# Hybrid decoder trunk: sums of weights formed in the first layer only, sums of h stored by GpSimd and loaded later, last weight pieces of the first layer at another priority

## The chip, the cores and the metric

The kernel runs on one core of a Trainium2 chip. The metric is the device time of one execution in microseconds (us), from the run's own timer; the value given is the median of several runs. The profile is of one more execution, recorded by the hardware profiler. PE is TensorE (matmuls), DVE is VectorE, ACT is ScalarE, POOL is GpSimd, and SP is SyncE, which here only issues DMA transfers. All five run their own list of instructions in order and wait for each other by semaphores.

## The reference

Two decoder layers on 512 tokens of width 1024, each followed by h = LayerNorm(alpha * h + sublayer(h)). In short:

```python
# layer 0 (even): one projection x @ w_in, cut into q, k, v, g_ret, xb, g_lru
ret = retention(rope(q), rope(k) * dk ** -0.5, v)        # 8 heads, per-head decay
ret = group_norm(ret) * gn_g + gn_b
ret = ret * silu(g_ret)
lru = rg_lru(causal_conv(xb)) * silu(g_lru)              # gated linear recurrence
y0 = concat([ret, lru]) @ w_out
# layer 1 (odd): h @ w_in, cut into q, k, v, g
p = softmax(q @ k.T, causal)                             # 8 heads, two maps each
out = (p1 - lam * p2) @ v
out = rms_norm(out) * subln_g * (1 - lambda_init) * silu(g)
y1 = out @ w_out
```

Everything is float32.

## The kernel before

**Precision.** Each float32 operand is split into a high part and a low part (`split`: a cast on ACT, a subtraction on DVE), and each product is three matmuls: high x high, high x low, low x high (`mm3`, L152). PE therefore runs some 4,255 matmuls, most of 128x128 by 128x512, and each weight piece needs a cast on ACT and a subtraction on DVE before PE can use it.

**Weight pieces.** The weights come in 162 pieces of 128x1024 (512 KB) in the order of use, w0, w1, and so on (`order`). `fetch` loads the next piece through SP into one of a few raw buffers (three in the first layer, four in the second), splits it into one of five pairs of buffers (the first two pieces of the second layer, w64 and w65, have a pair of their own each), and appends it to `ready`. `take(ahead)` returns the next piece and makes sure that `ahead` more have been fetched. w4 to w57 and v's pieces are projections of the first layer; w58 and w59 are the output projection of a retention pair ("ro"), and w60 to w63 of the last pairs ("eo"). w64 to w67 are the second layer's v, w68 to w71 its g, w72 to w79 its first q and k.

**Sums of weights.** In the second layer the gate and the value projections of head pairs 1 to 3 are done together by a scheme of Strassen's kind: seven products of half-size blocks in place of eight (`gates_values`). It needs sums of weight blocks, formed in HBM: for each, SP copies one block to `t` (L180), and GpSimd's queue adds another by a DMA that accumulates (L181). 24 sums of 128x1024, in halves of 64 rows, make 48 pairs of transfers. `fetch` issues one pair behind a weight piece n if `n >= SUM_FIRST and n % 3 != SUM_REST`, that is behind two pieces of three.

**Sums of h.** The same scheme needs four sums of blocks of h. `act_sums` makes them on DVE and ACT while PE does g of the second layer, and stores their high and low parts to HBM (`sd`, eight stores of 512 KB, L720). They are loaded later into `sx`, two at a time (`load_sum`, L743). `sx` shares its buffer with `y`, the residual sum, so that y is stored first (`store_y`, L701), `sx` loaded for a group, and y loaded again for the next output projection. The list `later` says when: `qk_unit` (one projection of a q or k, followed by its rope) takes one entry after each unit.

**Order.** PE's and SP's instructions stand in the order of the program text (`manual_schedule`), with side jobs (retention, recurrence, attention, layer norm) put between matmuls by `Side.tick`. The order on DVE, ACT and POOL is made by the compiler's scheduler, in which `tc.high_priority(n)` moves what is recorded inside it ahead by n. The pieces of the second layer's v are taken with priority `P_WEIGHTS` = 450 (L209).

**At the seam.** "eo" is the first layer's last output unit: for each of four row blocks, w60 and w61 with the recurrence's results (lrum3), then w62 and w63 with the retention's (retm3). After each row block, `even_end` does its layer norm on DVE, and later four by four transposes on PE (ht, L601) make h. Then come v (ov_ps), g (og_ps), and the units q00o, q01o, k00o, k01o, q10o and so on. Each is 24 matmuls.

Of the kernel before, what the change touches and what calls it, by code (L numbers as in the profile page):

```python
# [42 lines left out]
WARM_UP = 7  # L43
EARLY = 2

SUM_FIRST, SUM_ROWS, SUM_REST = 6, 64, 0

ATT_BUSY = 1

# [51 lines left out]
def trunk(ctx: ExitStack, tc: tile.TileContext, a):  # L101
    nc = tc.nc
# [64 lines left out]
    def fetch(parts=((0, D),)):  # L167
        if len(ready) < len(order):
            n = len(ready)
            src, scale = order[n]  # L170
            raw = raws[n % len(raws)].tile([P, D], F32, tag="raw", name=f"w{n}_r")
            w = pair(extra.pop(n, wsp), [P, D], "w", f"w{n}")
            for lo, hi in parts:
                c = slice(lo, hi)
                nc.sync.dma_start(out=raw[:, c], in_=src[:, c])
                split(raw[:, c], cut(w, ALL, c), scale=scale)
                yield
            if n >= SUM_FIRST and n % 3 != SUM_REST and sums:
                dst, one, two = sums.pop(0)
                nc.sync.dma_start(out=dst, in_=one)  # L180
                nc.gpsimd.dma_start(out=dst, in_=two, max_dma_last_dim=4 * D, accum_op=ALU.add)  # L181
            ready.append(w)
# [3 lines left out]
    def take(ahead):  # L186
        taken[0] += 1
        while len(ready) < min(taken[0] + ahead, len(order)):
            list(fetch())
        return ready[taken[0] - 1]  # L190

    def t_unit(act, name):
        w = take(2)
        ps = bank(ps_pj, "pj", name + "_ps")
        for kt in range(KT):
            mm3(ps, cut(w, ALL, slice(kt * P, kt * P + P)), cut(act, ALL, kt), kt == 0, kt == KT - 1)
            side.tick()
        return ps
# [25 lines left out]
                for sb, j in steps:  # L224
                    product(ps[sb], w, sb, 2 * i + j)

    def out_unit(mix, y, name, first, before=None, after=None, late=0):
        n = len(mix)
        w = [take(1 if n == 2 else 0) for _ in range(n)]
        y = y()  # L230

        step = 2 if n == 4 and after is None else 1
        for sbs in (range(i, i + step) for i in range(0, SB, step)):
            pss = {(sb, hf): bank(ps_pj, "pj", f"{name}_ps{sb}{hf}") for sb in sbs for hf in range(2)}
            steps = [(c, sb, hf) for c in range(0, n, 2) for sb in sbs for hf in range(2)]
            if late and sbs[0] == SB - 1:
                steps.sort(key=lambda t: t[2])
            for c, sb, hf in steps:
                if before is not None and hf == 0:
                    before(c // 2, sb)  # L240
                ps = pss[sb, hf]
                for i in range(c, c + 2):
                    mm3(ps, cut(mix[i], ALL, slice(sb * P, sb * P + P)), cut(w[i], ALL, slice(hf * HALF, hf * HALF + HALF)), i == 0, i == n - 1)
                    side.tick()
                if c < n - 2:
                    continue
                yy = y[:, sb, hf * HALF:hf * HALF + HALF]
                with tc.high_priority(late):
                    if first:
                        nc.vector.scalar_tensor_tensor(out=yy, in0=yy, scalar=ALPHA, in1=ps, op0=ALU.mult, op1=ALU.add)  # L250
                    else:
                        nc.vector.tensor_tensor(out=yy, in0=ps, in1=yy, op=ALU.add)  # L252
                    if late:
                        if hf == 0:
                            st = small.tile([P, 2, 6], F32, tag="bst", name="bst", bufs=2)
                        nc.vector.bn_stats(out=st[:, hf], in_=yy)
                        stats[sb] = st
                if after is not None and hf:
                    after(sb)
# [22 lines left out]
    sums = []  # L282
# [266 lines left out]
    def even_out(kinds, p, name, **kw):  # L549
        def before(c, sb):  # L550
            if sb == 0:
                for i in range(2):
                    side.need(job[kinds[c], 2 * p + i])

        out_unit([t for kind in kinds for t in mix_of(m.pop((kind, p)))], lambda: y, name, p == 0, before=before, **kw)
# [51 lines left out]

    hj = []
    gb0 = ln_params(a["ev_ln"], "ln0", (two, "dec"), (two, "dec"), (two, "gwh", 1), (two, "gwl", 1))
    even_out(("lru", "ret"), 3, "eo", after=even_end)  # L610


    phase.close()
# [92 lines left out]
    def act_sums():  # L706
        def block(r, c, x):
            return h[x][:, 4 * c:4 * c + 4, 2 * P * r:2 * P * r + 2 * P].bitcast(F32)

        def less(t, one, two, three):  # L710
            nc.vector.scalar_tensor_tensor(out=t, in0=one, scalar=-1.0, in1=two, op0=ALU.mult, op1=ALU.subtract)
            yield 2
            nc.vector.tensor_tensor(out=t, in0=t, in1=three, op=ALU.subtract)
            yield 1

        def put(n):
            split(low[n], (st[n][:, 0].bitcast(F32R), low[n].bitcast(F32R)))
            yield 3
            for x in range(2):
                nc.sync.dma_start(out=sd[n][:, x], in_=st[n][:, x])  # L720

        def difference(t, one, two):
            nc.vector.tensor_tensor(out=t, in0=block(*one, 0), in1=block(*two, 0), op=ALU.subtract)
            yield 2
            nc.vector.tensor_tensor(out=t, in0=t, in1=block(*one, 1), op=ALU.add)
            yield 1
            nc.vector.tensor_tensor(out=t, in0=t, in1=block(*two, 1), op=ALU.subtract)
            yield 2

        st = [ss.tile([P, 2, KT // 2, 2 * P], F32, tag=f"ss{n}", name=f"ss{n}") for n in range(4)]  # L730
        low = [t[:, 1] for t in st]
        yield from difference(low[0], (1, 1), (1, 0))
        yield from less(low[1], low[0], block(0, 0, 0), block(0, 0, 1))
        yield from put(0)
        yield from less(low[3], low[1], block(0, 1, 0), block(0, 1, 1))
        yield from put(1)
        yield from put(3)
        yield from difference(low[2], (0, 0), (1, 0))
        yield from put(2)
# [81 lines left out]
                for qb in range(SB):  # L821
                    side.need(oj[hd, qb])

    later, busy = [], [0]

    def no_op():
        pass

    def swap_in():
        nonlocal sx  # L830
# [1 line left out]
        load_sum(1, 0)  # L832
        load_sum(2, 1)

    def qk_unit(n, name):
        r = rope(t_unit(h, name), n, name)
        if later:
            later.pop(0)()
        return r

    sx = None
# [2 lines left out]
    for kind, i in od:  # L844
        if kind == "v":
            vs[i] = []

            def evac(sb, ps):
                past(i - 1)
                t = pair(vp, [P, S], "v", f"ov{i}{sb}")  # L850
                split(ps, t)
                vs[i].append(t)

            s_unit(h, f"ov{i}", i == 0, evac, lambda sb: side.need(hj[sb]))
            vt[i] = side.now + ATT_VALUE
            if i == 0:
                early.close()
                scratch = ctx.enter_context(ExitStack())
                ss = pool("ss", 1, scratch)
                summed = side.add(act_sums(), "sums", 1)  # L860
        elif kind == "g":
            def evac(sb, ps):
                past(i - 1)
                if sb % 2 == 0:
                    pairs[sb] = gp.tile([P, 2, S], F32, tag="g", name=f"og{i}{sb}")
                gates[sb, i] = pairs[sb - sb % 2][:, sb % 2]
                silu2(ps, gates[sb, i], work(f"og{i}{sb}_t"))

            pairs = {}
            s_unit(h, f"og{i}", False, evac)  # L870
            side.need(summed)
            scratch.close()
            qkp = pool("qkp2", 4)
            es = pool("es2", 2)
            mask = load("mask", [P, S], a["mask"], pl=es, bufs=1)
            later[:] = [store_y, no_op, swap_in]
        elif kind == "gv":
            gates_values(i)
        elif kind == "qk":
            om[i] = mix_pair(f"om{i}") if i < 7 else None  # L880
            qk = [[qk_unit(n, f"{n}{i}{mp}o") for mp in range(2)] for n in "qk"]
            om[i] = om[i] or cut(pair(big, [P, KT, S], "x", "om7"), ALL, slice(0, 2))
            for qb in range(SB):
                oj[i, qb] = side.add(attention(i, qb, *qk, om[i]), "att", 3, ATT_START[i], ATT_GAP[i])
        else:
            odd_out(i, f"oo{i[0]}")
            if i[0] < 4:
                later[:] = [store_y, no_op, swap_in]
    gb1 = ln_params(a["od_ln"], "ln1", *((qkp, n) for n in ("qh", "ql", "kh", "kl")))
    odd_out((6, 7), "oo6", after=odd_end, late=P_LAST)  # L890

# [82 lines left out]
```

## Time and profile before

| | us |
|---|---|
| median of 3 runs (941.3 to 943.25) | 942.57 |
| the profiled execution, its own time | 941.73 |
| its span, first to last instruction | 939.9 |
| idle time of PE up to 360 us (of 340 from 20) | 1.6 |
| longest wait of PE for another engine | 2.7 |

The profile page gives, for each engine, busy time and share; further views group instructions by line, list who waited for whom, or show one engine's instructions in order of time. In such a row the first number is the start in us from the span's start, the second the duration, then follow engine, line, operation, written tile <- read tiles and shapes; a bracket at the end tells how long the engine was idle before it and what ended that. A view by stretches gives each engine's busy time in a part of the span, with the clock that TensorE was granted (1.00 is full) and the share of time in which the DMA engines were busy.

### The profile page before, as it was taken

To read this page: it belongs to the slowest core of one execution; us is meant where nothing else is said; L and a number is where in the kernel's file an instruction comes from. 1 tells how busy PE (TensorE), PEld (TensorE's weight loads), DVE (VectorE), ACT (ScalarE), POOL (GpSimd) and SP (SyncE) were. 2 spreads that over 40 slices of the span, in tenths; PEclk is the share of its full clock that TensorE was granted. 3 is DMA by queue.
4 is the path that set the end of the run, shared out by engine and by line. 5 is a ranking of instruction groups with operands and counts; after the bars stand their busy time and mean duration, and the time that the engine had idled before them with its cause. 6 is when DMAs were issued, how large, how long until landed. Compare 5 with 4: busy or idle time off the path is not lost.

```text
span 939.9 us, 11808 instructions
## 1 busy us (share of the span) xinstructions
PE 913.0 (97%) x4255; PEld 751.7 (80%) x4255; DVE 745.6 (79%) x1243; ACT 477.2 (51%) x780; POOL 103.2 (11%) x160
## 2 busy tenths in 40 slices
PE   9999999999999999899999999999999999999996
PEld 7888888878888788678877888878788788887885
DVE  5887997868778987997669987749877578878787
ACT  5467786556384776432325455423455333664230
POOL 0110000100101010120002120000120100201113
PEclk9999999999999999999999999999999999999999
DMA  7885353833837363840894216546247382278002
GB/s 247 249 266 146 119 140 101 253 94 124 212 97 205 105 168 110 236 124 23 302 335 137 88 67 224 217 152 236 72 140 255 132 297 95 71 268 284 24 1 89
DMA packets 46522, 152.92 MB, mean 163 GB/s; under 512 B 6144, under 2 KB 6272, under 8 KB 45696
## 3 DMA queue, kind: packets, MB, share of 16 engines
q1 hardware_dynamic: 42624, 139.59, 42.1%
q0 software_dynamic: 3840, 12.59, 8.4%
q8 instruction: 33, 0.54, 0.2%
q14 instruction: 25, 0.20, 0.1%
HBM read 139.57 MB, written 37.75 MB: 189 GB/s over the span
## 4 chain that ended last, share of the span: by engine, by line
PE 67%; DVE 16%; ACT 6%; DMA 5%; issue 2%; POOL 2%; SPq 1%; POOLq 0%; DVEq 0%; ACTq 0%
PE oo_ps L155 2%; PE oo_ps L154 2%; PE oo_ps L153 2%; DMA w_r<-in_od_w 2%; PE out_ps L153 2%; PE out_ps L155 2%; PE out_ps L154 2%; PE xb_ps L154 1%; PE xb_ps L155 1%; PE xb_ps L153 1%; PE q_ps L153 1%; PE q_ps L155 1%; PE q_ps L154 1%; DMA w_r<-in_ev_w 1%; PE gr_ps L155 1%
## 5 line engine op out<-in xcount | busy, mean ns | idle before, releaser
L638 ACT ACTIVATE e<-as,nm 128x128 f32<-128x128 f32 (+3 forms) x64 | 33.2, 523 | 39.3 <-DVE nm L635 39.3
L181 POOL DMA_DIRECT2D t<-t x24 | 18.9, 786 | 243.1 <-DMA t<-in_od_w 243.1
L645 POOL TENSOR_SCALAR zr<-z 128x1 f32<-128x1 f32 x32 | 17.8, 557 | 241.0 <-ACT e L638 241.0
L671 DVE SCALAR_TENSOR_TENSOR o<-po,ars,og 128x256 f32<-128x256 f32 x32 | 15.5, 484 | 35.6 <-POOL ars L349 35.5
L181 POOL DMA_DIRECT2D t<-in_od_w x24 | 19.1, 796 | 190.6 <-DMA t<-in_od_w 190.6
L635 DVE CUSTOM_DVE_ANT_0 as<-as,mask 128x128 f32<-128x128 f32 (+3 forms) x64 | 30.5, 507 | 2.0 <-PE as L155 1.9
L668 POOL TENSOR_SCALAR ave<-ss,zr 128x1 f32<-128x1 f32 x32 | 16.1, 503 | 126.5 <-ACT po L665 118.5
L665 ACT ACTIVATE po<-po 128x256 f32<-128x256 f32 x32 | 12.0, 375 | 29.6 <-PE po L155 26.1
L349 POOL TENSOR_TENSOR ars<-ave,nhalf 128x1 f32<-128x1 f32 x32 | 20.0, 625 | 2.7
L646 DVE SCALAR_TENSOR_TENSOR e<-e,zr,e 128x128 f32<-128x128 f32 (+3 forms) x32 | 17.6, 550 | 0.8
L506 DVE SCALAR_TENSOR_TENSOR xc<-xbp,vecs,xc 128x509 f32<-128x509 f32 (+2 forms) x24 | 17.9, 747 | 0.2
L463 DVE TENSOR_TENSOR rsd<-rs,dec 128x512 f32<-128x512 f32 (+3 forms) x32 | 15.5, 486 | 3.1 <-PE rs L155 3.0
L252 DVE TENSOR_TENSOR y<-oo_ps,y 128x512 f32<-128x512 f32 x24 | 16.1, 684 | 2.1 <-PE oo_ps L155 2.0
L650 PE MATMUL wt<-ident,e 128*128 128x128 f32 x80 | 14.1, 274 | 1.8 <-DVE e L646 1.6
L149 ACT CAST hh<-ht 128x512 fp32r<-128x512 f32 x8 | 4.7, 587 | 21.7 <-PE ht L601 21.7
L650 PEld LDWEIGHTS wt<-ident,e 128*128 128x128 f32 x80 | 10.2, 140 | 6.5 <-DVE e L646 2.7
L675 PEld LDWEIGHTS po<-ident,o 128*128 128x128 f32 x64 | 8.6, 140 | 5.4 <-DVE o L671 1.9
L522 DVE TENSOR_TENSOR xbp<-xbp,xc 128x512 f32<-128x512 f32 x8 | 5.5, 690 | 9.3 <-ACT xbp L519 9.3
L528 DVE SCALAR_TENSOR_TENSOR xc<-t,r 128x512 f32<-128x512 f32 x8 | 5.5, 691 | 9.0 <-ACT r L527 8.9
L675 PE MATMUL po<-ident,o 128*128 128x128 f32 x64 | 12.4, 275 | 0.2
L638 ACT ACTIVATION_READ_ACCUMULATOR e<-as,nm 128x1 f32 x64 | 12.5, 196 | 0.0
L432 ACT ACT_TABLE_LOAD x9 | 11.5, 1283 | 0.2
(2845 smaller groups left out, 3468.7 us busy)
## 6 DMA issues: line engine op xcount, KB each, us to landing
w_r<-in_od_w SPq DMA_DIRECT2D x58, 512.0 KB, 6.0
w_r<-in_ev_w SPq DMA_DIRECT2D x47, 512.0 KB, 5.1
t<-in_od_w SPq DMA_DIRECT2D x48, 256.0 KB, 5.5
sx<-sd SPq DMA_DIRECT2D x24, 512.0 KB, 5.4
w_r<-t SPq DMA_DIRECT2D x24, 512.0 KB, 3.4
w_r<-in_ev_wo SPq DMA_DIRECT2D x16, 512.0 KB, 5.1
w_r<-in_od_wo SPq DMA_DIRECT2D x16, 512.0 KB, 4.6
t<-in_od_w POOLq DMA_DIRECT2D x24, 256.0 KB, 5.1
```

Source lines behind the costliest of these rows:

```text
L153: nc.tensor.matmul(out=out, lhsT=l[0], rhs=r[0], start=start, stop=False, **kw)
L154: nc.tensor.matmul(out=out, lhsT=l[0], rhs=r[1], start=False, stop=False, **kw)
L155: nc.tensor.matmul(out=out, lhsT=l[1], rhs=r[0], start=False, stop=stop, **kw)
L181: nc.gpsimd.dma_start(out=dst, in_=two, max_dma_last_dim=4 * D, accum_op=ALU.add)
L349: nc.gpsimd.tensor_tensor(out=out, in0=var, in1=nhalf[:, :1], op=ALU.pow)
L506: nc.vector.scalar_tensor_tensor(out=xc[:, sh:], in0=xb[:, :S - sh], scalar=conv_w(w, c), in1=xc[:, sh:], op0=ALU.mult, op1=ALU.add)
L635: nc.vector.tensor_tensor_reduce(out=ps[:, :n], in0=ps[:, :n], in1=mask[:, S - n:], scale=-QK_SCALE, scalar=3.0e38, op0=ALU.add, op1=ALU.m ...
L638: nc.scalar.activation(out=e, in_=ps[:, :n], func=AF.Exp, scale=-1.0, bias=nm, accum_out=z[:, mp:mp + 1])
L645: nc.gpsimd.tensor_scalar(out=zr[:, 1:2], in0=z[:, 0:1], scalar1=z[:, 0:1], scalar2=EPS, op0=ALU.mult, op1=ALU.mult)
L646: nc.vector.scalar_tensor_tensor(out=ee[0], in0=ee[1], scalar=zr[:, 0:1], in1=ee[0], op0=ALU.mult, op1=ALU.add)
L650: nc.tensor.transpose(out=pt[:, kb * P:kb * P + P], in_=ee[0][:, kb * P:kb * P + P], identity=ident)
L675: nc.tensor.transpose(out=pm[:, i * P:i * P + P], in_=o[:, i * P:i * P + P], identity=ident)
```

## The change

Four edits:

1. The sums of weights are issued behind eight pieces of nine (`n % 9`) in place of two of three. The 48 pairs of transfers then stand behind pieces w6 to w59, all in the first layer, instead of w7 to w77.
2. The stores of the sums of h are issued by GpSimd instead of SP.
3. `later` is a table by unit: y is stored after the first q or k unit as before, and `sx` is loaded after the sixth instead of the third.
4. The last output unit of the first layer takes w60 to w63 (as far as they haven't been fetched) with priority `P_WEIGHTS`.

```diff
-SUM_FIRST, SUM_ROWS, SUM_REST = 6, 64, 0
+SUM_FIRST, SUM_ROWS, SUM_REST = 6, 64, 9
+Y_OUT, Y_IN = 0, 5
...
-            if n >= SUM_FIRST and n % 3 != SUM_REST and sums:
+            if n >= SUM_FIRST and n % SUM_REST and sums:
...
-    def out_unit(mix, y, name, first, before=None, after=None, late=0):
+    def out_unit(mix, y, name, first, before=None, after=None, late=0, early=0):
         n = len(mix)
-        w = [take(1 if n == 2 else 0) for _ in range(n)]
+        with tc.high_priority(early):
+            w = [take(1 if n == 2 else 0) for _ in range(n)]
...
-    even_out(("lru", "ret"), 3, "eo", after=even_end)
+    even_out(("lru", "ret"), 3, "eo", after=even_end, early=P_WEIGHTS)
...
-                nc.sync.dma_start(out=sd[n][:, x], in_=st[n][:, x])
+                nc.gpsimd.dma_start(out=sd[n][:, x], in_=st[n][:, x])
...
-    later, busy = [], [0]
-
-    def no_op():
-        pass
+    later, units, busy = {}, 0, [0]
...
+    def swap():
+        nonlocal units
+        units = 0
+        later.update({Y_OUT: store_y, Y_IN: swap_in})
+
     def qk_unit(n, name):
+        nonlocal units
         r = rope(t_unit(h, name), n, name)
-        if later:
-            later.pop(0)()
+        if units in later:
+            later.pop(units)()
+        units += 1
         return r
...
-            later[:] = [store_y, no_op, swap_in]
+            swap()
...
-                later[:] = [store_y, no_op, swap_in]
+                swap()
```

The order on PE is the same in both kernels. In the changed file all lines from L45 on lie 2 to 7 lines further down. Three places where other engines' orders differ:

SP, at the start of the second layer, before; w are weight pieces, t sums of weights, sd stores of the sums of h, yd stores of y, sx loads of the sums of h:

```order
L175 DMA w72_r_3990<-in_od_w 128x1024
L720 DMA sd1_3707<-ss1_3921 128x1024 x2
L720 DMA sd3_3709<-ss3_3923 128x1024 x2
L175 DMA w73_r_4029<-in_od_w 128x1024
L180 DMA t321_114<-in_od_w 16x4096
L720 DMA sd2_3708<-ss2_3922 128x1024 x2
L159 DMA mask_4086<-in_mask 128x512
L175 DMA w74_r_4090<-in_od_w 128x1024
L180 DMA t321_114<-in_od_w 16x4096
L701 DMA yd0_3456<-y_201 128x1024
```

After three more stores of y come w75, w76, a sum, the four loads of sx, and w77. The same place in the changed kernel:

```order
L177 DMA w72_r_3998<-in_od_w 128x1024
L177 DMA w73_r_4037<-in_od_w 128x1024
L161 DMA mask_4092<-in_mask 128x512
L177 DMA w74_r_4096<-in_od_w 128x1024
L704 DMA yd0_3480<-y_201 128x1024
```

and, after the other stores of y:

```order
L177 DMA w75_r_4141<-in_od_w 128x1024
L177 DMA w76_r_4182<-in_od_w 128x1024
L177 DMA w77_r_4223<-in_od_w 128x1024
L177 DMA w78_r_4266<-in_od_w 128x1024
L177 DMA w79_r_4307<-in_od_w 128x1024
L746 DMA sx_4370<-sd1_3727 128x2x512 x2
L746 DMA sx_4370<-sd2_3728 128x2x512 x2
```

The sums and the stores sd are gone from this queue (the stores stand on POOL now), and the loads of sx stand behind w79 instead of w76.

DVE, at the first layer's last output unit, before; rq is the last retention head on its way to its result retm3, y the residual sum, ls a small reduction, bst a row block's layer norm:

```order
L495 TENSOR_TENSOR rq_3346<-rq_3346,gr_3305 128x512
L252 TENSOR_TENSOR y<-ro_ps_3436,y 128x512
L252 TENSOR_TENSOR y<-ro_ps_3437,y 128x512
L150 TENSOR_TENSOR retm3l<-rq_3346,retm3h 128x512
L150 TENSOR_TENSOR w65l<-w_r,w65h 128x1024
L150 TENSOR_TENSOR w63l<-w_r,w63h 128x1024
L618 TENSOR_TENSOR lq<-lq 128x256
L620 TENSOR_REDUCE ls<-lq 128x2
L252 TENSOR_TENSOR y<-eo_ps_3490,y 128x512
```

and in the changed kernel:

```order
L152 TENSOR_TENSOR w63l<-w_r,w63h 128x1024
L152 TENSOR_TENSOR w65l<-w_r,w65h 128x1024
L498 TENSOR_TENSOR rq_3370<-rq_3370,gr_3329 128x512
L255 TENSOR_TENSOR y<-ro_ps_3461,y 128x512
L623 TENSOR_REDUCE ls<-lq 128x2
L152 TENSOR_TENSOR retm3l<-rq_3370,retm3h 128x512
L626 SCALAR_TENSOR_TENSOR nlam<-ls 128x1
L255 TENSOR_TENSOR y<-eo_ps_3510,y 128x512
```

The splits of w63 and w65 moved from behind retm3l to a place ahead of the product with the gate (gr) that makes retm3; one sum into y moved up past them, and the product of lq further up.

DVE, at the first attention block, before; as and e are scores and softmax of head 0, q10o and q11o rope steps of head 1:

```order
L635 ISA as_4332,nm<-as_4332,mask 128x128
L635 ISA nm 128x1
L150 TENSOR_TENSOR w79l<-w_r,w79h 128x1024
L635 ISA as_4340,nm<-as_4340,mask 128x128
L635 ISA nm 128x1
L150 TENSOR_TENSOR q10ol<-q10o_c,q10oh 128x512
L150 TENSOR_TENSOR w80l<-w_r,w80h 128x1024
L643 RECIPROCAL zr<-z 128x1
L332 TENSOR_TENSOR q11o_c<-q11o_ps,cos 128x512
L644 TENSOR_SCALAR zr<-zr,z,nlam 128x1
L335 TENSOR_TENSOR q11o_s<-q11o_ps,sin 64x512
L646 SCALAR_TENSOR_TENSOR e_4338<-e_4346,zr,e_4338 128x128
```

and in the changed kernel:

```order
L638 ISA as_4327,nm<-as_4327,mask 128x128
L638 ISA nm 128x1
L638 ISA as_4335,nm<-as_4335,mask 128x128
L638 ISA nm 128x1
L152 TENSOR_TENSOR q10ol<-q10o_c,q10oh 128x512
L646 RECIPROCAL zr<-z 128x1
L647 TENSOR_SCALAR zr<-zr,z,nlam 128x1
L649 SCALAR_TENSOR_TENSOR e_4333<-e_4341,zr,e_4333 128x128
L335 TENSOR_TENSOR q11o_c<-q11o_ps,cos 128x512
```

The splits w79l and w80l have moved to places further up, and the rope steps of q11o stand behind the softmax step (e) instead of between its parts.

## The prediction

> **What bounds the kernel now.** The page comes first, then stretches of the span.
>
> ```profile
> span 939.9 us, 11808 instructions
> PE 913.0 (97%) x4255; PEld 751.7 (80%) x4255; DVE 745.6 (79%) x1243; ACT 477.2 (51%) x780; POOL 103.2 (11%) x160
> ```
>
> PE is busy 97% of the span, and its own order of instructions is the same in both kernels: the change can only shorten or lengthen PE's waits. All of PE's idle time is 939.9 - 913.0 = 26.9 us, which caps any gain, apart from slow clock. The view by stretches says where it lies (stretch, its length, busy PE, PEld, DVE, ACT, POOL with counts, granted clock, DMA share, GB/s).
>
> ```profile
> 20.00:360.00 340.00, 338.43 (x1526) 279.52 (x1525) 281.29 (x430) 222.65 (x291) 28.43 (x36) 1.00 0.56 160
> 380.00:400.00 20.00, 17.31 (x76) 13.68 (x75) 18.11 (x30) 7.75 (x10) 3.27 (x4) 1.00 0.77 230
> 400.00:420.00 20.00, 18.52 (x90) 15.05 (x89) 18.58 (x32) 6.14 (x8) 4.35 (x5) 1.00 0.48 123
> 448.00:492.00 44.00, 41.98 (x178) 33.91 (x177) 29.11 (x36) 13.01 (x18) 3.16 (x4) 0.96 0.96 335
> 500.00:520.00 20.00, 18.60 (x94) 14.84 (x93) 18.13 (x39) 9.54 (x23) 4.81 (x6) 1.00 0.40 129
> ```
>
> Up to 360 us PE idles 1.6 us in 340, with the DMA engines at 0.56. The waits sit around the seam of the two layers: 2.7 us, 1.5 us, 2.0 us (DMA at 0.96, clock below 1) and 1.4 us. These are the places that the change reaches.
>
> **Part 1: no sums, no stores of h's sums and a later load in SP's queue (448 to 492).** PE there (start, duration, instruction; in brackets idle time and its releaser), and last a narrow stretch for the clock:
>
> ```profile
> 474.62 0.39 PE L154 MATMUL k00o_ps<-hl,w74h 128*128 128x512 f32 x1
> ...
> 477.56 0.39 PE L155 MATMUL k00o_ps<-hh,w74l 128*128 128x512 f32 x1
> 478.55 0.50 PE L153 MATMUL k01o_ps<-hh,w75h 128*128 128x512 f32 x1 [0.59 <-ACT w75h L149]
> ...
> 480.70 0.50 PE L155 MATMUL k01o_ps<-hh,w75l 128*128 128x512 f32 x1 [1.42 <-DVE w75l L150]
> ...
> 485.14 0.39 PE L155 MATMUL k01o_ps<-hh,w75l 128*128 128x512 f32 x1
> 482.00:484.00 2.00, 2.00 (x7) 1.52 (x6) 1.31 (x3) 0.62 (x1) 0.00 (x0) 0.50 0.97 321
> ```
>
> The 13 steps from 474.62 to 477.56 take 0.226 us each. The 15 steps from 477.56 to 485.14 should take 3.39 us and take 7.58: **4.19 us lost**, some 2.4 to the late piece w75 and 1.8 to the clock, which falls to 0.50 behind that wait. Why w75 is late:
>
> ```profile
> 448.98 6.24 SPq L720 DMA_DIRECT2D sd<-ss  x4
> 465.64 0.98 SPq L175 DMA_DIRECT2D w_r<-in_od_w  x2
> 475.33 3.03 SPq L743 DMA_DIRECT2D sx<-sd  x4
> 442.30 1.22 DVE L150 TENSOR_TENSOR w71l<-w_r,w71h 128x1024 fp32r<-128x1024 f32 x1
> 477.45 1.05 ACT L149 CAST w75h<-w_r 128x1024 fp32r<-128x1024 f32 x1 [1.42 <-DMA w_r<-in_od_w]
> ```
>
> SP issues in order. It stands at the stores of h's sums, whose operands DVE is still making, then issues four stores of y, and w75 only at 465.64, into full DMA engines; it lands 11.8 us later. In the changed order w72 to w75 stand ahead of everything that waits for DVE's sums. What releases w75 is then its buffer, which the split of w71 ends at 442.30 + 1.22 = 443.5. Even with 11.8 us to landing it is there at 455, over 20 us before PE wants it. The sums that are issued here (DMA issues of 440 to 500: count, size each, us to landing) are gone too, 2 MB of the stretch's 44 x 0.335 = 14.7 MB:
>
> ```profile
> t<-in_od_w SPq DMA_DIRECT2D x4, 256.0 KB, 9.3
> t<-t POOLq DMA_DIRECT2D x4, 256.0 KB, 7.3
> ```
>
> Term: **-4.2**; bounds 0 (w75 as late as now) and -4.2. On the clock, the Trainium skill, "TensorE: Matmul & The Clock Gate", Part 1, has the half rate come after an idle window of about 3.4 us. By that rule waits of 0.59 and 1.42 us would cost no clock and the sum below would be 1.8 us smaller; this trace shows the clock fall behind them, and does not show it fall behind 2.66 us at 393, so the measurement decides.
>
> **Part 2: the last pieces w60 to w63 with the next layer's priority (374 to 409).**
>
> ```profile
> 382.90 1.03 ACT L149 CAST w64h<-w_r 128x1024 fp32r<-128x1024 f32 x1
> 386.63 1.05 ACT L149 CAST w63h<-w_r 128x1024 fp32r<-128x1024 f32 x1 [2.69 <-PE ro_ps L155]
> 390.02 0.68 DVE L150 TENSOR_TENSOR retm3l<-rq,retm3h 128x512 fp32r<-128x512 f32 x1
> 391.47 1.23 DVE L150 TENSOR_TENSOR w65l<-w_r,w65h 128x1024 fp32r<-128x1024 f32 x1 [0.76 <-ACT w65h L149]
> 393.88 0.50 PE L154 MATMUL eo_ps<-w63l,retm3h 128*128 128x512 f32 x1 [2.66 <-DVE w63l L150]
> 406.89 2.72 DVE L378 SCALAR_TENSOR_TENSOR y<-y,lrs,ln 128x512 f32<-128x512 f32 x4
> 407.68 0.66 PE L601 MATMUL ht<-ident,y 128*128 128x128 f32 x4 [1.49 <-DVE y L378]
> ```
>
> PE waits 2.66 us for w63l, which stands behind w65l on DVE. The change puts w63l ahead of w65l; but w63h still waits for the last ro_ps matmul at 386.6 (its buffer), and both splits now stand ahead of the gate product that makes retm3, with w65h ahead of retm3h on ACT. PE wants retm3 about a microsecond before this wait begins (393.88 - 2.66 = 391.2), near 390.2. Counted on: w64h is cast one short step earlier than at 382.90, so w64l ends near 384.5. Eight DVE steps stand between it and w63l, 0.6 to 0.7 us each (four take 2.72 in the row of L378): 389.4. Two splits, whose starts lie 1.14 apart in the rows, the product 0.6, a sum into y 0.6, a short reduction 0.4 and retm3l 0.7: near 394, where w63l ends now. So I expect **another wait, for retm3, of about the same length: 0**. Bounds: -2.7 (retm3 in time) and +1 (w65 lands a microsecond after DVE reaches its split, and all of this stands behind it). Further on, DVE's order now has the second step of the first row block's layer norm (L378) right behind w66l instead of behind the next two blocks. From 394, with eight short steps, one split and PE's sums to wait for, it would end near 402; the transposes that wait 1.49 us for it come at 406. Term: **-1.5**, bounds -1.5 and 0 (DVE has no idle time in this stretch to give). One more wait stands ahead of these (waits of PE, then ACT):
>
> ```profile
> PE rv L480 <- ACT rq7h L149: 0.9, 1, 0.9
> 374.26 1.05 ACT L149 CAST w61h<-w_r 128x1024 fp32r<-128x1024 f32 x1 [6.43 <-DMA w_r<-in_ev_wo]
> ```
>
> rq7h stands behind w61h on ACT, before and after. The sum copies between the loads of w61 to w63 go, and w61 may land sooner: 0, bounds -0.9 and 0.
>
> **Part 3: the first attention block (500).**
>
> ```profile
> 497.33 1.22 DVE L150 TENSOR_TENSOR w79l<-w_r,w79h 128x1024 fp32r<-128x1024 f32 x1
> 499.28 1.22 DVE L150 TENSOR_TENSOR w80l<-w_r,w80h 128x1024 fp32r<-128x1024 f32 x1
> 502.51 0.33 PE L650 MATMUL wt<-ident,e 128*128 128x128 f32 x1 [1.09 <-DVE e L646]
> ```
>
> Here DVE catches up with late pieces between the steps of the softmax that PE waits for. In the changed order w79l and w80l are done before, and q11o's first rope steps come behind: two splits of 1.14 us less ahead of a wait of 1.09. Term: **-1.1**, bounds -1.1 and 0.
>
> **Part 4: what is added.** Ten more sums, of two transfers each, in the first layer. They meet DMA engines at 0.56; the tightest piece there beyond the start:
>
> ```profile
> 138.98 1.22 DVE L150 TENSOR_TENSOR w24l<-w_r,w24h 128x1024 fp32r<-128x1024 f32 x1
> 144.91 0.40 PE L154 MATMUL out_ps<-w24l,retm0h 128*128 128x512 f32 x1
> ```
>
> It is ready at 140.2, 4.7 us before use. A 256 KB copy at the 335 GB/s above takes 0.8 us. Term: 0; if the cover were gone, ten times 0.8 would be 8. The eight stores go to POOL:
>
> ```profile
> q1 hardware_dynamic: 42624, 139.59, 42.1%
> q0 software_dynamic: 3840, 12.59, 8.4%
> L181 POOL DMA_DIRECT2D t<-in_od_w x24: 778/781/1016, 33.7 to 418.4; - x24
> 451.38 3.49 DVE L150 TENSOR_TENSOR ss<-ss 128x1024 fp32r<-128x1024 f32 x3
> ```
>
> POOL spends 0.78 us on 64 rows, so 0.78 to 1.56 on 128, at most 13 us in all, with nothing else to do until 498. The stores' 4.2 MB need 12 us at q1's pace (139.59 MB in 0.421 x 939.9 us) and 26 us at q0's (12.59 MB in 0.084 x 939.9), so from 444, when the first is ready, they land by 456 to 470. The first rope result's cast, q00oh, waits for all of them and is due near 468: k01o is due at 477.8, q00o's unit is the third before it and ends two units of 24 x 0.226 us earlier, at 466.9, less the lead of 1.5, plus four rope steps. Behind it stand on ACT w78h, on DVE q00ol and the next rope; PE reaches what these hold up only at q11o (a rival below). Term: 0.
>
> The two later loads of sx are each moved past three weight pieces in SP's queue; PE has no wait for a piece there, and two more projections and two products stand ahead of the first product that reads sx: 0.
>
> **Sum**, against the profiled execution (941.73 us, 0.84 below the median of 942.57): -4.2 - 1.5 - 1.1 = -6.8, so 934.9; from the median **935.8**.
>
> **Rivals.**
> *POOL's stores are late (slower).* PE feels q00oh when q11o needs the PSUM bank that q01o's rope empties:
>
> ```profile
> 492.89 0.39 PE L153 MATMUL q11o_ps<-hh,w77h 128*128 128x512 f32 x1
> ```
>
> That is 487 with the lead of 5.7 us, and the cast, q00ol and three rope steps take 3.4: stores landing after about 484 decide it. At q0's pace halved by shared engines they land at 444 + 53 = 497: 13 us lost, 949. For it: q0 moves 159 GB/s against q1's 353. Against it: q0's traffic adds into memory, these stores do not. The Trainium skill, "SBUF - State Buffer", "Two separate sides", warns of this change: VectorE in its two-port modes keeps GpSimd from writing descriptors, 3.1 us for 0.62. The row of POOL's issues does not agree: at most 1.02 us beside a DVE busy 79%. 5%.
> *The first layer pays.* The sums delay pieces whose casts hold up ACT: 5 to 8 us given back, 941 to 944, about no change. Slack of 4.7 us and more speaks against it. 7%.
> *The seam stays full.* As many bytes but the sums still move, and w75 is late in any case: only 2.6 gained, 940. 5%.
>
> **Numbers.** The forecast, with its bounds, has 83%: from 6.8 + 2.7 + 1 = 10.5 gained (932) to 4.2 - 1 = 3.2 (939.4). With a microsecond for the spread of the runs the range is **931.2 to 940.2**. 0.2% (1.9 us) is about what a measurement can tell from no change. Faster: 83 plus most of the full seam, 87%. Same: 8%. Slower: 5%.
>
> **What would show it.** Right: no wait of k01o for w75 and clock 1.00 around 480; the wait of ht gone; q00oh soon after its rope. At w63 a wait of some 2.7 us, now for retm3. Wrong: clock dips or waits of ACT for w pieces in 100 to 360, or q00oh waiting for DMA over 15 us.

## The result, and the profile after

| | before | changed |
|---|---|---|
| median, us | 942.57 (5 runs, 941.30 to 943.25) | 933.53 (5 runs, 931.89 to 934.14) |
| span of the profiled execution, us | 939.9 | 931.8 |

The ratio is 0.9902, with a 95% interval of 0.9887 to 0.9916: 9.0 us less by the medians, 8.1 by the spans. (Run again on another occasion, the changed kernel took 933.82 us, 0.9920 [0.9904, 0.9936] of the kernel before.)

The page of the changed kernel:

```profile
span 931.8 us, 11817 instructions
PE 909.9 (98%) x4255; PEld 750.3 (81%) x4255; DVE 746.2 (80%) x1243; ACT 477.6 (51%) x780; POOL 105.2 (11%) x168
```

Its view by stretches, columns as in the prediction:

```profile
20.00:360.00 340.00, 338.50 (x1528) 279.95 (x1527) 281.47 (x426) 222.86 (x291) 37.94 (x48) 1.00 0.62 177
380.00:400.00 20.00, 17.95 (x71) 13.80 (x70) 17.58 (x29) 7.10 (x10) 0.94 (x1) 0.91 0.36 129
400.00:420.00 20.00, 20.00 (x99) 16.56 (x98) 19.45 (x33) 6.17 (x9) 1.92 (x2) 1.00 0.16 56
448.00:492.00 44.00, 44.00 (x199) 36.52 (x198) 36.64 (x47) 15.56 (x19) 2.97 (x6) 1.00 0.62 230
500.00:520.00 20.00, 19.89 (x100) 16.36 (x99) 17.99 (x37) 9.39 (x23) 3.57 (x8) 1.00 0.15 53
```

The first layer paid nothing for ten more sums: PE is busy 338.50 of 340 us, with the DMA engines at 0.62 in place of 0.56. From 448 to 492 PE has no idle time left, the clock is 1.00 and the DMA share fell from 0.96 to 0.62. At 400 to 420 and 500 to 520 the idle time went from 1.5 to 0 and from 1.4 to 0.1. Only 380 to 400 didn't gain: its clock is now 0.91.

Since PE's order is the same in both kernels, each matmul can be paired with itself. Rows of PE at places that the prediction doesn't show, before:

```profile
375.21 0.39 PE L155 MATMUL ro_ps<-w59h,retm2l 128*128 128x512 f32 x1
376.50 0.50 PE L480 MATMUL rv<-rq7h,ones 128*128 128x512 f32 x1 [0.91 <-ACT rq7h L149]
396.51 0.39 PE L153 MATMUL eo_ps<-w61h,lrum3h 128*128 128x512 f32 x1
509.59 0.44 PE L650 MATMUL wt<-ident,e 128*128 128x128 f32 x2 [0.18 <-DVE e L646]
672.19 0.39 PE L153 MATMUL po<-ov10h,w31h 128*128 128x256 f32 x1 [0.40 <-DVE om3l L150]
797.98 0.39 PE L153 MATMUL po<-ov20h,w51h 128*128 128x256 f32 x1 [0.40 <-DVE om5l L150]
```

and the same matmuls in the changed kernel, with those of the prediction's rows at 393, 407.68, 485.14 and 502.51:

```profile
374.14 0.39 PE L157 MATMUL ro_ps<-w59h,retm2l 128*128 128x512 f32 x1
375.83 0.50 PE L483 MATMUL rv<-rq7h,ones 128*128 128x512 f32 x1 [1.31 <-ACT rq7h L151]
392.12 0.50 PE L155 MATMUL eo_ps<-w63h,retm3h 128*128 128x512 f32 x1 [1.91 <-ACT retm3h L151]
396.98 0.40 PE L155 MATMUL eo_ps<-w61h,lrum3h 128*128 128x512 f32 x1
406.53 0.60 PE L604 MATMUL ht<-ident,y 128*128 128x128 f32 x4
479.74 0.39 PE L157 MATMUL k01o_ps<-hh,w75l 128*128 128x512 f32 x1
495.63 0.27 PE L653 MATMUL wt<-ident,e 128*128 128x128 f32 x1
502.33 0.38 PE L653 MATMUL wt<-ident,e 128*128 128x128 f32 x2
664.34 0.39 PE L155 MATMUL po<-ov10h,w31h 128*128 128x256 f32 x1
789.69 0.38 PE L155 MATMUL po<-ov20h,w51h 128*128 128x256 f32 x1
```

Two rows of DVE in the changed kernel, the gate product ahead of retm3 and the layer norm's second step ahead of ht, and the clock behind the wait at 392:

```profile
390.73 0.68 DVE L498 TENSOR_TENSOR rq<-rq,gr 128x512 f32<-128x512 f32 x1
400.21 1.41 DVE L381 SCALAR_TENSOR_TENSOR y<-y,lrs,ln 128x512 f32<-128x512 f32 x2
392.00:394.00 2.00, 1.74 (x5) 1.12 (x6) 1.48 (x5) 0.27 (x2) 0.00 (x0) 0.88 0.02 4
394.00:396.00 2.00, 2.00 (x6) 1.60 (x5) 0.94 (x3) 0.00 (x0) 0.00 (x0) 0.50 0.96 305
396.00:398.00 2.00, 2.00 (x8) 1.58 (x8) 1.90 (x5) 1.05 (x1) 0.01 (x1) 0.77 0.92 352
```

The lead is the start before minus the start now. What it gains from one place to the next is what that place gave:

| place | lead, us | gained there | predicted |
|---|---|---|---|
| end of the projections, 375.21 to 374.14 | 1.07 | 1.07 | none |
| rv behind rq7h, 376.50 to 375.83 | 0.67 | -0.40 | 0 |
| eo behind w63l, now retm3h, 396.51 to 396.98 | -0.47 | -1.14 | 0 |
| ht, 407.68 to 406.53 | 1.15 | 1.62 | 1.5 |
| k01o, 485.14 to 479.74 | 5.40 | 4.25 | 4.2 |
| first attention block, 509.59 to 502.33 | 7.26 | 1.86 | 1.1 |
| om3l and om5l, 797.98 to 789.69 | 8.29 | 1.03 | 0 |

Why w75 is in time, in SP's, ACT's and POOL's rows of the changed kernel (the last is a group: count, shortest, median and longest duration in ns, first and last start):

```profile
442.36 16.56 SPq L177 DMA_DIRECT2D w_r<-in_od_w  x5
459.13 6.07 SPq L746 DMA_DIRECT2D sx<-sd  x4
455.05 1.05 ACT L151 CAST w75h<-w_r 128x1024 fp32r<-128x1024 f32 x1 [1.45 <-PE og_ps L157]
469.92 0.62 ACT L151 CAST q00oh<-q00o_c 128x512 fp32r<-128x512 f32 x1 [3.16 <-DVE q00o_c L340]
L723 POOL DMA_DIRECT2D sd<-ss x8: 531/533/618, 442.6 to 456.3; - x8
```

w75 is cast at 455.05, not 477.45, and ACT waited there for PE, not for a DMA. q00oh starts when DVE has its operand; from 448 to 492 PE has no wait that could lead back to GpSimd's eight stores.

### The profile page after: what moved, and what is told of

Same layout as the page of the kernel before. It is cut to its first block, busy times and chain, and to the rows that moved or that the text cites. A ratio compares the mean times of both kernels' runs of the same rounds, so it can differ in the third digit from the quotient of the medians.

```text
span 931.8 us, 11817 instructions
## 1 busy us (share of the span) xinstructions
PE 909.9 (98%) x4255; PEld 750.3 (81%) x4255; DVE 746.2 (80%) x1243; ACT 477.6 (51%) x780; POOL 105.2 (11%) x168
## 4 chain that ended last, share of the span: by engine, by line
PE 78%; DVE 11%; ACT 5%; issue 2%; POOL 2%; DMA 1%; SPq 0%; POOLq 0%; DVEq 0%; ACTq 0%
PE oo_ps L155 2%; PE oo_ps L157 2%; PE oo_ps L156 2%; PE out_ps L155 2%; PE out_ps L157 2%; PE out_ps L156 2%; PE xb_ps L156 1%; PE xb_ps L155 1%; PE xb_ps L157 1%; PE ev_ps L156 1%; PE ev_ps L157 1%; PE ev_ps L155 1%; PE gr_ps L157 1%; PE gr_ps L156 1%; PE k_ps L157 1%
## 5 line engine op out<-in xcount | busy, mean ns | idle before, releaser
L648 POOL TENSOR_SCALAR zr<-z 128x1 f32<-128x1 f32 x32 | 15.1, 472 | 264.9 <-ACT e L641 264.9
L352 POOL TENSOR_TENSOR lrs<-lve,nhalf 128x1 f32<-128x1 f32 x8 | 7.3, 912 | 85.0 <-DVE lve L365 85.0
L653 PEld LDWEIGHTS wt<-ident,e 128*128 128x128 f32 x80 | 10.4, 140 | 4.1 <-PE gv1a L157 0.8
```

The source lines that it names most:

```text
L352: nc.gpsimd.tensor_tensor(out=out, in0=var, in1=nhalf[:, :1], op=ALU.pow)
L653: nc.tensor.transpose(out=pt[:, kb * P:kb * P + P], in_=ee[0][:, kb * P:kb * P + P], identity=ident)
```

## The experiments

Ten runs, each timed in five rounds against the kernel before. First each edit was undone alone, then each of the first three was made alone. A run's ratio is to the kernel before on the same occasion: 941.32 us for the first four rows, 942.06 for the next four, 940.92 for the last two. The changed kernel's own two ratios, 0.9902 and 0.9920, lie 1.7 us apart, so smaller differences between rows are not clear of noise.

| kernel | median, us | ratio [95%] |
|---|---|---|
| changed, edit 1 undone | 932.97 | 0.9908 [0.9892, 0.9924] |
| changed, edit 2 undone | 934.67 | 0.9925 [0.9909, 0.9940] |
| changed, edit 3 undone | 936.96 | 0.9949 [0.9933, 0.9964] |
| changed, edit 4 undone | 933.59 | 0.9908 [0.9893, 0.9924] |
| before, with edit 1 alone | 935.00 | 0.9927 [0.9912, 0.9942] |
| before, with edit 2 alone | 940.43 | 0.9977 [0.9967, 0.9988] |
| before, with edit 3 alone | 940.38 | 0.9982 [0.9970, 0.9994] |
| changed, early gate product | 930.85 | 0.9883 [0.9867, 0.9898] |
| changed, once more | 933.82 | 0.9920 [0.9904, 0.9936] |
| edits 1 and 4, early gate product | 932.92 | 0.9914 [0.9899, 0.9929] |

**Edit 1 undone**

```diff
-SUM_FIRST, SUM_ROWS, SUM_REST = 6, 64, 9
+SUM_FIRST, SUM_ROWS, SUM_REST = 6, 64, 3
```

> The changed kernel with edit 1 undone: the sums of weights again stand behind two pieces of three (to w77), the other three edits stay. Theory A (the late w75 came from SP standing at the stores of h's sums, edit 2): SP no longer stands there, so k01o's wait stays away and this kernel keeps most of the gain, 7 to 9 of the 9.0 us over the kernel before: 933.5 to 935.5 us. Rival B (w75 was late because the sums' bytes filled the DMA engines): k01o waits again and the clock dips behind it, 2.4 to 4.2 us are lost: 936 to 938 us. If the 1.1 us gained in the later groups (om3, om5) came from the absence of sums in the second layer, they are still gained here, since before had none there either.

Nothing lost: 932.97 us. k01o doesn't wait; w75 is cast at 455.74. So the sums' bytes alone did not make w75 late. But two places of the seam changed sides. The wait for retm3 is gone: in DVE's list the gate product (388.05) now stands ahead of the splits of w63 (388.65) and w65 (391.15). And ht waits again, 2.03 us, and the clock falls behind it. Rows of PE and DVE, and a stretch:

```profile
405.56 0.66 PE L604 MATMUL ht<-ident,y 128*128 128x128 f32 x4 [2.03 <-DVE y L381]
404.77 2.72 DVE L381 SCALAR_TENSOR_TENSOR y<-y,lrs,ln 128x512 f32<-128x512 f32 x4
408.00:410.00 2.00, 2.00 (x6) 1.57 (x5) 1.58 (x4) 0.44 (x1) 0.00 (x0) 0.50 0.84 131
```

The layer norm's second step of the first block stands behind the second block's first step again, though edit 4 is in. Its place therefore hangs on the sums, not on the priority of w60 to w63.

**Edit 2 undone**

```diff
-                nc.gpsimd.dma_start(out=sd[n][:, x], in_=st[n][:, x])
+                nc.sync.dma_start(out=sd[n][:, x], in_=st[n][:, x])
```

> The changed kernel with edit 2 undone: the eight stores of the sums of h are issued by SP again, between w71 and w75; the other three edits stay. Theory A (SP standing at these stores delays w72 to w75): w75h stands on ACT behind q00oh again, k01o waits for w75 with the clock dip behind the wait, and the wt wait of the first attention block returns: 3 to 5 us lost, 936.5 to 938.5 us. Rival B (the sums' bytes alone): no wait of k01o, 933 to 934.5 us, as the changed kernel.

Theory A's mechanism came back without its price. SP stands at the stores again, and w75 is cast behind q00oh, on a DMA:

```profile
470.03 1.05 ACT L151 CAST w75h<-w_r 128x1024 fp32r<-128x1024 f32 x1 [0.58 <-DMA w_r<-in_od_w]
```

That is still 5.5 us ahead of k01o, which starts at 475.48 without a wait. What the trace shows of a cost is one wait of 1.0 us for om0l near 506, with the splits of w73 to w81 later in DVE's list. 934.67 us is about 1 us above the changed kernel's two medians; the ratio, 0.9925, is not clear of that kernel's 0.9902 and 0.9920.

**Edit 3 undone**

```diff
-Y_OUT, Y_IN = 0, 5
+Y_OUT, Y_IN = 0, 2
```

> The changed kernel with edit 3 undone: sx is loaded after the third q or k unit again, ahead of three weight pieces more; the other three edits stay. The record priced this edit at 0. Theory A (the waits of po for om3l and om5l that went, some 1.1 us together, went because of the later load, which moves the splits of w107, w108 and w133, w134 on DVE): 0.8 to 1.5 us lost, 934.3 to 935 us, and waits of 0.5 us and more for om3l and om5l are back. Rival B (they went for another reason, or by chance of one profile): 933 to 934 us.

936.96 us, the largest loss of the four, at both places that theory A names. Rows of SP, ACT, DVE and PE, and one of the list of PE's waits (om5l has the same):

```profile
454.15 10.44 SPq L746 DMA_DIRECT2D sx<-sd  x4
470.92 1.05 ACT L151 CAST w77h<-w_r 128x1024 fp32r<-128x1024 f32 x1 [9.86 <-DMA w_r<-in_od_w]
472.00 1.22 DVE L152 TENSOR_TENSOR w77l<-w_r,w77h 128x1024 fp32r<-128x1024 f32 x1 [4.22 <-ACT w77h L151]
507.55 0.39 PE L155 MATMUL po<-ov00h,w01h 128*128 128x256 f32 x1 [1.01 <-DVE om0l L152]
PE po L155 <- DVE om3l L152: 0.4, 1, 0.4
```

With w75 and w76 early, SP reaches the loads of sx at 454 and stands there for 10.4 us. GpSimd issues the last store of the same data at 455.4, and these stores land up to 8.0 us after their issue, so that SP most likely waits for them. w77 stands behind them, and q00oh behind w77h on ACT (471.87). In the changed kernel DVE splits w77 at 468.01:

```profile
468.01 1.23 DVE L152 TENSOR_TENSOR w77l<-w_r,w77h 128x1024 fp32r<-128x1024 f32 x1
```

From there to om0l DVE's list is the same in both but for one swap (w77l and q00o_c); it only runs late. Its steps from w78's split to om0l start 1.7 to 2.4 us after those of the changed kernel, though PE is 0.9 us ahead of that kernel's at 490. So PE waits for DVE, at the softmax (1.2 us in all) and at om0l.

**Edit 4 undone**

```diff
-    even_out(("lru", "ret"), 3, "eo", after=even_end, early=P_WEIGHTS)
+    even_out(("lru", "ret"), 3, "eo", after=even_end)
```

> The changed kernel with edit 4 undone: w60 to w63 are taken with no added priority; the other three edits stay. On DVE, w65l and retm3l then stand ahead of w63l, and w66l ahead of the first row block's layer norm. Theory A (by the lead of the trace: ht's wait of 1.5 us returns, the wait for w63l of 2.7 us takes the place of 1.9 us for retm3 and the half clock behind it, 1.7 us): between 0.5 us faster and 1.5 us slower than the changed kernel, 933 to 935 us; the clock near 394 is 1.00. Rival B (w66l, which stands at DMA until 397, now holds up DVE's layer norm): ht waits 2.5 us or more, 935 to 937 us.

933.59 us, no difference. The wait at 392 is for w63l again, 2.2 us, and the clock stays at 1.00 behind it. ht does not wait, against both theories: edit 4 isn't what removed that wait.

**Edit 1 alone**

```diff
-            if n >= SUM_FIRST and n % 3 != SUM_REST and sums:
+            if n >= SUM_FIRST and n % SUM_REST and sums:
```

(with `SUM_REST` = 9)

> The kernel before with edit 1 alone (all sums in the first layer). Theory A, from the runs that undid one edit: sums and stores of h's sums together made w75 late, so that taking either out of SP's queue is enough: k01o no longer waits (2.4 us, 4.2 with the clock behind it), and ht's wait of 1.5 us goes too, since it was gone in the run without edit 4: 3.5 to 6 us faster than before. Rival B (SP's standing at the stores is what counts, edit 2 needed): less than 1.5 us faster.

935.00 us, 7.1 us below before and more than expected. Theory A holds in both parts, in DVE's and ACT's rows:

```profile
398.49 1.40 DVE L376 SCALAR_TENSOR_TENSOR y<-y,bmv,ln 128x512 f32<-128x512 f32 x2
399.81 1.41 DVE L378 SCALAR_TENSOR_TENSOR y<-y,lrs,ln 128x512 f32<-128x512 f32 x2
470.64 1.05 ACT L149 CAST w75h<-w_r 128x1024 fp32r<-128x1024 f32 x1 [0.93 <-DMA w_r<-in_od_w]
```

The second step of the layer norm follows the first at once and ht has no wait; w75 is 5 us ahead of k01o.

**Edit 2 alone**

```diff
-                nc.sync.dma_start(out=sd[n][:, x], in_=st[n][:, x])
+                nc.gpsimd.dma_start(out=sd[n][:, x], in_=st[n][:, x])
```

> The kernel before with edit 2 alone (the stores of h's sums by GpSimd). Theory A: k01o no longer waits for w75, which stands on ACT ahead of q00oh: 2.4 to 4.2 us faster than before; ht still waits 1.5 us or more, and w63l's wait stays. Rival B (the sums' bytes count, edit 1 needed): less than 1.5 us faster. A third possibility: POOL's accumulating transfers stand behind the stores in its queue, t's last sums and with them the loads of sx come late: slower than before.

940.43 us, 1.6 us faster. k01o's wait is gone (w75 is cast at 457.50), but of a lead of 3.15 us at 490 only some 0.9 is left at 517, as where edit 3 was undone. Rows of SP, ACT and PE:

```profile
458.20 11.10 SPq L743 DMA_DIRECT2D sx<-sd  x4
475.57 1.05 ACT L149 CAST w77h<-w_r 128x1024 fp32r<-128x1024 f32 x1 [11.14 <-DMA w_r<-in_od_w]
512.20 0.39 PE L153 MATMUL po<-ov00h,w01h 128*128 128x256 f32 x1 [1.02 <-DVE om0l L150]
```

**Edit 3 alone**

```diff
-            later[:] = [store_y, no_op, swap_in]
+            later[:] = [store_y, no_op, no_op, no_op, no_op, swap_in]
```

(at both places)

> The kernel before with edit 3 alone (sx loaded after the sixth unit). Theory A: undone alone the edit cost 3.3 us in the trace, 1.6 of it at 495 to 506 (waits for e and om0l) and 1.7 at 590, 664 and 790; alone it gives the 1.7 of the later groups at least: 1.7 to 3.3 us faster than before, with k01o's wait as it was. Rival B (it pays only where the other edits have brought w77 to w79 forward): less than 0.7 us faster.

940.38 us, 1.7 us faster, the lower end of theory A. k01o waits as before, 2.12 us, with the half clock behind it. om3l's and om5l's waits are gone:

```profile
671.25 0.39 PE L153 MATMUL po<-ov10h,w31h 128*128 128x256 f32 x1
796.58 0.39 PE L153 MATMUL po<-ov20h,w51h 128*128 128x256 f32 x1
```

**The changed kernel with the last gate product early**

```diff
-        nc.vector.tensor_tensor(out=n1, in0=n1, in1=gates.pop(("gr", h)), op=ALU.mult)
-        split(n1, cut(m, ALL, h % 2))
+        with tc.high_priority(400) if h == 7 else ExitStack():
+            nc.vector.tensor_tensor(out=n1, in0=n1, in1=gates.pop(("gr", h)), op=ALU.mult)
+            split(n1, cut(m, ALL, h % 2))
```

> The changed kernel with one more priority: the last head's gate product and the split that makes retm3 are recorded with priority 400, so that DVE does them ahead of w65l. Theory A (what is left at 392 is DVE's order alone): the wait of 1.9 us for retm3 and the half clock that stood behind it in one profile go: 1.5 to 3.5 us faster than the changed kernel, 930 to 932 us, 1.1 to 1.3 per cent under before. Rival B (w66l now stands ahead of the first row block's layer norm and waits for its piece, so that ht waits in its place): 932.5 to 934 us, ht waits 1 to 3 us.

930.85 us (930.33 to 931.60): every run is below every run of the changed kernel, by 2.7 to 3.0 us at the medians and 1.8 to 3.5 by the ratios. DVE's rows, and a stretch:

```profile
389.06 0.69 DVE L498 TENSOR_TENSOR rq<-rq,gr 128x512 f32<-128x512 f32 x1
389.66 1.22 DVE L152 TENSOR_TENSOR w63l<-w_r,w63h 128x1024 fp32r<-128x1024 f32 x1
390.80 0.69 DVE L152 TENSOR_TENSOR retm3l<-rq,retm3h 128x512 fp32r<-128x512 f32 x1
391.40 1.23 DVE L152 TENSOR_TENSOR w65l<-w_r,w65h 128x1024 fp32r<-128x1024 f32 x1
392.00:394.00 2.00, 2.00 (x11) 1.63 (x10) 2.00 (x4) 0.00 (x0) 0.00 (x0) 1.00 0.66 203
```

The wait at 392 is gone and no new one took its place: ht still starts without a wait, 3.1 us earlier.

**The changed kernel once more**

> The changed kernel itself once more, on the same chip as the next run. Theory A (the half clock behind a wait of about 2 us comes by chance of phase, in some executions of the same instructions and not in others): 932 to 934.5 us; the wait of 1.9 us for retm3 stands in the profile again, while the clock behind it may be 0.5 for some 3.4 us or 1.00 throughout. Rival B (it belongs to this order of instructions): the clock falls again at 392 to 397.

The wait for retm3 is 1.87 us, and the clock fell behind it again. Up to 400 us the run without edit 2 has the same instructions in the same order on every engine, and waits the same 1.87 us at the same place. The stretch from 394 to 396, in this run and then in that one:

```profile
394.00:396.00 2.00, 2.00 (x5) 1.63 (x6) 1.22 (x2) 0.00 (x0) 0.00 (x0) 0.50 0.57 154
```

```profile
394.00:396.00 2.00, 2.00 (x11) 1.62 (x10) 1.91 (x3) 0.00 (x0) 0.00 (x0) 1.00 0.68 242
```

So neither the order of the instructions nor the length of the wait decides the dip: rival B falls. Whether it is chance of phase, as theory A says, isn't shown.

**Edits 1 and 4 with the early gate product, edits 2 and 3 undone**

The edit is that of the early gate product, with those of the second and third runs.

> Edits 1 and 4 with the early gate product, edits 2 and 3 undone: sums in the first layer, stores of h's sums by SP, sx loaded after the third unit. Theory A (edit 1 carries k01o, ht and most of the first attention block by itself, the early gate the wait at 392; edits 2 and 3 add only the later groups' 1.1 us and some 0.5 around 500 to 520): 1 to 2 us slower than with all four edits and the early gate (930.9), 932 to 933 us. Rival B (edits 2 and 3 are needed): 934 us and more.

932.92 us, as theory A has it: two of the four edits and the early gate product reach the changed kernel's time. Edits 2 and 3 add 2 to 3 us more, by the medians and by the ratios. Part of the difference in the profiles is another dip of the clock, here behind the wait for rq7h:

```profile
376.45 0.49 PE L483 MATMUL rv<-rq7h,ones 128*128 128x512 f32 x1 [1.31 <-ACT rq7h L151]
378.00:380.00 2.00, 2.00 (x7) 1.52 (x6) 2.00 (x4) 1.97 (x3) 0.00 (x0) 0.50 0.55 217
```

## Why the prediction held, point by point

**Part 1, -4.2.** It gave 4.25, wait and clock together. The mechanism was right, but more was made of it than was needed. The prediction took the stores and the sums together. The runs show that w75 was late only with both in SP's queue: with either taken out, w75 is cast at 455 to 471, ahead of k01o at 475.5 to 479. With edit 3 alone it is cast at 477.28 and the wait stays.

**Part 2, the wait for w63l.** "Another wait, for retm3, of about the same length: 0" was right in kind. Its working was not: it has PE ask for retm3 near 390.2 and get it near 394, which would be a wait of 3.8 us. PE ran the three products of w62 with retm3 from 389.37, before retm3h was cast at 391.45. They read the half of retm3 that head 6 had made, and only w63 needs head 7's. The wait went from 2.66 to 1.91 us, and PE then stood some 0.3 us for retm3l. The term is mis-sized by the clock, which fell behind the shorter wait and cost about 1.7 us: a loss of 1.14 in all, just outside the bound of 1. The wait itself was an order of DVE's and no bound of the data, as the early gate product shows: 1.9 us, and the clock where it falls, were to be had.

**Part 2, ht, -1.5.** It gave 1.62. That the layer norm's second step would follow w66l at once was right (400.21, ending at 401.6), but the cause that was told is wrong. The prediction put it down to the priority of w60 to w63. With edit 4 undone the wait stays away, with edit 1 undone it returns, with edit 1 alone it goes. In all four profiles with the sums spread over both layers ht waits 1.49 to 2.03 us, in all eight with the sums in the first layer it doesn't. So the step moved because the sums were gone from this stretch. Why the scheduler orders DVE so is only argued: GpSimd makes `lrs`, which that step reads, and the sums' transfers stood between its steps.

**Part 2, rq7h, 0.** It lost 0.4: w61 landed sooner by the clock (w61h at 373.58, not 374.26), but PE was 1.07 us ahead by then and waited longer for it. In the other profiles this wait is 0.8 to 1.3 us with either placing of the sums, so that one profile tells nothing here.

**Part 3, -1.1.** It gave 1.86 up to 509.59: 1.48 by the first row (wt at 502.51) and 0.38 by the next block. The step was right (w79l and w80l out of the way of the softmax). From 490 to 509.59 all four edits gain 1.8 us, edit 1 alone 1.1 and edit 3 alone 1.2. With edit 1 undone nothing of the 1.8 is lost; with edit 3 undone 1.0 is, and another 1.5 right behind, at om0l.

**Part 4, sums and stores, 0.** Right. The rivals of a paying first layer and of late stores fell: q00oh waits for its operand, and the stores land in 4.8 us (median). They took GpSimd 0.53 us each (0.62 at most), below the 0.78 to 1.56 that the prediction allowed, beside a DVE that was busy 17.0 us of 17 from 440 on. The danger was near, though by another way than the rival told: stores from GpSimd with sx loaded early make SP stand 10 to 11 us ahead of w77. With edit 2 alone that took back some 2.2 of the 4.2 us that k01o had given in the profile.

**Part 4, the later loads of sx, 0.** This term failed. It asked whether PE waits for a piece, and not what a late piece does to ACT and DVE: SP stands at the loads of sx, the next piece lands late, and what stands behind its cast and split, the ropes and the attention, comes late with it. For the first group the rows of the run without edit 3 show this. In the later groups DVE's list changes in the same way in the changed kernel and with edit 3 alone: the splits of w107 to w109 move up, and the last rope step of q40o stands ahead of two score steps instead of between them. How that makes om3l 0.4 us earlier was not followed further. The edit is worth 1.03 us in the two later groups, and 3.1 to 3.4 us by the medians where the other edits are in.

**The 1.07 us ahead of 375** belong to no edit. They come from the first 25 us: there the first profile of the changed kernel is 1.0 us ahead of the one before, and the second, of the same kernel, 0.1 us behind it. So the sum of 6.8 was met by 8.1 in the spans partly by luck, with two errors that nearly cancel: 1.1 for the clock behind retm3 against 1.07 at the start. What remains is the 1.0 of the later groups and 0.8 of the first attention block, less 0.4 at rq7h.

## What to carry to other kernels

When a piece of data comes late at the end of a queue, list all that stands ahead of it. Here either of two causes could be taken away with the same effect, so edits made together don't add up: alone, edits 1, 2 and 3 gave 7.1, 1.6 and 1.7 us, together with the fourth 9.0. Where a store moves to another engine's queue, look for the load that reads it back: it now waits in the first queue, ahead of everything behind it. And a wait that stays after an edit may be only the order of one in-order engine; raise the work that PE wants next, not only the work that was seen to be late.

## What the runs showed of the hardware

**The half clock behind short waits.** Behind the wait at 392 (1.87 to 2.66 us) the granted clock fell to 0.50 in four of nine profiles that have it: behind 1.91, 1.87, 2.39 and 2.08 us, but not behind another 1.87, 1.90, 2.21, 2.22 and 2.66 us. It also fell behind 1.31 us (rq7h, edits 1 and 4 with the early gate product), 2.03 us (ht, edit 1 undone) and 2.12 us (k01o, edit 3 alone), but not behind 1.31 us for rq7h in the changed kernel. Each time it cost about 1.7 us (in the changed kernel the clock is 0.88, 0.50 and 0.77 in the three stretches of 2 us from 392: 0.24 + 1.00 + 0.46). The length of the wait doesn't decide it. The Trainium skill ("TensorE: Matmul & The Clock Gate", Part 1) has the half rate come after an idle window of about 3.4 us; none of these waits is that long. What decides stayed open. Such dips are about as large as the spread of a kernel's runs (931.89 to 934.14 us), so that one profile can hold a term of 1.7 us that the next one lacks.

**Issuing on GpSimd.** A plain store of 128 rows took it 0.53 us, less than the 0.78 us of an accumulating transfer of 64 rows.
